# Decays of a gated DeltaNet layer from differences of running sums, with the rows spread by DMA and masked by GpSimd

## The chip, the cores and the metric

One core of a Trainium2 chip runs the whole kernel in one launch. Its engines run their own instruction streams, each in order: TensorE (PE, with its weight loads as PEld), VectorE (DVE), ScalarE (ACT), GpSimd (POOL) and SyncE (SP), which here only issues transfers. The metric is the device time of one execution in microseconds (us), as the median of several runs.

## The reference

The input is x (256 tokens by 2048 features, float32). Two layers follow, each h = h + Mixer(RMSNorm(h)). The first is a gated DeltaNet layer with 16 heads of 128, the second a chunked attention with a band of nine chunks of 64 and a relative bias. The change touches the decays of the first:

```python
beta = sigmoid(b_in)
g = -exp(a_log) * softplus(a_in + dt_bias)     # a gate per token and head
gc = cumsum(g)                                 # the reference restarts it in chunks of 64
decay = exp(where(tri_incl, gc[..., :, None] - gc[..., None, :], -inf))
lower = where(tri_strict, (k * beta) @ k.T * decay, 0)
qk = (q @ k.T) * decay
```

Decays therefore depend only on differences of the running sums of g. The kernel works on blocks of 128 tokens: for each head it holds three 128x128 blocks of decays, from tokens of the first half to the first half, from the first half to the second, and from the second half to the second. The first and the last are zero on the wrong side of the diagonal.

## The kernel before

Nearly all of the time goes into four projections. Their weights are read once, in a `plan` of 320 chunks of 512 KB. For each chunk, `fetch` issues a DMA from SP into a buffer `wt` (four of them); ACT rounds it to `whi` (L209, three buffers), and DVE takes the rest, `wlo` = `wt` - `whi` (L210, three buffers). PE then multiplies with both (L259): in a chunk of the kind "half", eight matmuls of 512 columns with `whi` and eight of 256 columns with `wlo`, and every second chunk starts with `wlo`. `fetch` runs up to three chunks ahead of use (`LOOK = 3`), but a cast into `whi` can start only when PE has finished with the buffer three chunks back.

All other work is written as generators (`decays`, `conv`, `q_conv`, `q_rest`, `k_small`, `inversion` and so on), put into two lists, `bgq` and `bg2`. After a certain number of matmuls, `step` advances one of them by one `yield`. From the resulting program, a scheduler with a timeline model then sets the order on each engine when the kernel is built; on the chip that order is fixed.

`decays` runs on `bg2` during the projection of q (from 33 to 109 us in the profile). It computes beta and the gates g (`q` in the code, 128 tokens by 16 heads by 2 halves). Then it forms the running differences as matrix products. DVE multiplies a 128x128 lower triangle `lt_f` by g for each head into `rbuf` (L486), in a rounded part and a rest (`g_r`, `gl_r`, made at L475 and L476). PE multiplies these with a strict triangle `gt_r` or with ones, `ones_r` (L501): three products for each of four groups of heads, each in two parts of 512 columns. ACT takes the exponentials out of PSUM into `dec`, a part of the tile `dl` (L506, L507 in width 512, L509 in width 128 with `tail`, the last column of the first block, as bias), and DVE multiplies the two diagonal blocks by the triangle (L516).

In `q_rest`, PE transposes q by heads (L552), after a silu on ACT (L546), and ACT sums the squares (L558). `conv` scales on ACT (L527) and adds three taps on DVE (L529).

Of the kernel before, what the change touches and what calls it, by code (L numbers as in the profile page):

```python
# [7 lines left out]
F32 = mybir.dt.float32  # L8
F32R = mybir.dt.float32r
BF16 = mybir.dt.bfloat16  # L10
AF = mybir.ActivationFunctionType
ALU = mybir.AluOpType
AX = mybir.AxisListType

P = 128
D = 2048
T = 256
H = 16
KT = D // P
EPS = 1e-6  # L20
NEG = -1e30
# [18 lines left out]
def tile_hybrid_trunk(  # L40
# [11 lines left out]
    nc = tc.nc  # L52
    act, dve, pool, pe = nc.scalar, nc.vector, nc.gpsimd, nc.tensor

    const = ctx.enter_context(tc.tile_pool(name="const", bufs=1))
# [3 lines left out]
    tiny = ctx.enter_context(tc.tile_pool(name="tiny", bufs=2))  # L59
# [3 lines left out]
    def ps_small():  # L63
        return pss.tile([P, 512], F32, name="pss", tag="pss")
# [5 lines left out]
    def slot(tag, kb, dt=F32):  # L70

        return big.tile([P, kb * 256], dt, name=tag, tag=tag)
# [5 lines left out]
    abm = slot("kT", 16)  # L78
# [5 lines left out]
    ps = ps_small()  # L84
    for _ in range(NWARM):
# [6 lines left out]
                       pattern=[[-1, P]], channel_multiplier=1)  # L92
    lt_f = abm[:, 1024:1024 + P]
    pool.memset(lt_f, 1.0)
    pool.affine_select(out=lt_f, in_=lt_f, compare_op=ALU.is_ge, fill=0.0, base=0,
                       pattern=[[1, P]], channel_multiplier=-1)
    gt_f = abm[:, 1024 + P:1024 + 2 * P]
    pool.memset(gt_f, 1.0)
    pool.affine_select(out=gt_f, in_=gt_f, compare_op=ALU.is_gt, fill=0.0, base=0,
                       pattern=[[-1, P]], channel_multiplier=1)  # L100
    ones_f = const.tile([P, P], F32, name="ones_f")
    pool.memset(ones_f, 1.0)
    nhalf = const.tile([P, 16], F32, name="nhalf")
    pool.memset(nhalf, -0.5)
    gt_r = const.tile([P, P], F32R, name="gt_r")
    ones_r = const.tile([P, P], F32R, name="ones_r")

    def rsqrt(dst, src, scale, bias):

# [298 lines left out]
    def ht(name, dt=F32):  # L408
        return const.tile([P, H, 2], dt, name=name)

    beta, g_r, gl_r = ht("beta"), ht("g_r", F32R), ht("gl_r", F32R)

    dl = slot("dl", 48).rearrange("p (h k c) -> p h k c", h=H, k=2)
    dec = dl[:, :, 1, :]
# [3 lines left out]
        return dl[:, 4 * k:4 * k + 4, 0, :].rearrange("p h (b d) -> p h b d", d=P)[:, :, 0::2, :]  # L418

    def decays():  # L420
        act.copy(out=gt_r, in_=gt_f)
        act.copy(out=ones_r, in_=ones_f)

        abr = slot("tt", 16, F32R)[:, :KT * 64 + 64]
        abv = abr[:, :KT * 64].rearrange("p (j a c) -> p j a c", a=2, c=32)
        act.copy(out=abr[:, KT * 64:], in_=ident[:, :64])
# [4 lines left out]
        ps = ps_small()  # L431
# [9 lines left out]
        ps = ps_small()  # L441
# [7 lines left out]
        for t in range(2):  # L449
            dve.tensor_scalar(out=ab[:, :, t], in0=ab[:, :, t], scalar1=rx[:, t:t + 1],  # L450
                              scalar2=None, op0=ALU.mult)

        y, ay, e, z, w2, q, eb = (abm[:, 1600 + 32 * i:1632 + 32 * i].rearrange("p (h t) -> p h t", t=2)
                                  for i in range(7))
# [13 lines left out]
        for n in (15, 13, 11, 9, 7, 5, 3):  # L468
# [3 lines left out]
        dve.scalar_tensor_tensor(out=q, in0=q, scalar=2.0, in1=y, op0=ALU.mult, op1=ALU.add)  # L472
        dve.scalar_tensor_tensor(out=q, in0=q, scalar=-1.0, in1=nea.unsqueeze(2).broadcast_to([P, H, 2]),
                                 op0=ALU.mult, op1=ALU.mult)
        dve.tensor_copy(out=g_r, in_=q)  # L475
        dve.tensor_tensor(out=gl_r, in0=q, in1=g_r.bitcast(F32), op=ALU.subtract)  # L476
        yield 1
        dve.tensor_scalar(out=eb, in0=eb, scalar1=1.0, scalar2=None, op0=ALU.add)
        dve.reciprocal(out=beta, in_=eb)

        rbuf = slot("tt", 16, F32R).rearrange("p (b k c) -> p b k c", b=2, k=4)

        def rhs(gi):
            for half in range(2):
                for part, src in ((0, g_r), (1, gl_r)):
                    dve.tensor_tensor(  # L486
                        out=rbuf[:, gi % 2, 2 * half + part, :].rearrange("p (h c) -> p h c", h=4),
                        in0=lt_f.unsqueeze(1).broadcast_to([P, 4, P]),
                        in1=src[:, 4 * gi:4 * gi + 4, half].bitcast(F32).unsqueeze(2).broadcast_to([P, 4, P]),
                        op=ALU.mult)  # L490

        rhs(0)
        yield 1
        rhs(1)
        yield 1
        for gi in range(4):
            hs = slice(4 * gi, 4 * gi + 4)
            ps3 = [ps_small() for _ in range(3)]
            for dst, lhs, half in ((ps3[0], gt_r, 0), (ps3[1], ones_r, 1), (ps3[2], gt_r, 1)):
                for part in range(2):  # L500
                    pe.matmul(dst, lhsT=lhs, rhs=rbuf[:, gi % 2, 2 * half + part, :],  # L501
                              start=(part == 0), stop=(part == 1))
            v0 = ps3[0].rearrange("p (h c) -> p h c", h=4)
            tail = tiny.tile([P, 4], F32, name="tail", tag="tail")
            dve.tensor_copy(out=tail, in_=v0[:, :, P - 1])
            act.activation(out=dec[:, hs, 0:128], in_=v0, func=AF.Exp)  # L506
            act.activation(out=dec[:, hs, 256:384], in_=ps3[2].rearrange("p (h c) -> p h c", h=4), func=AF.Exp)  # L507
            for i in range(4):
                act.activation(out=dec[:, 4 * gi + i, 128:256], in_=ps3[1][:, i * P:(i + 1) * P], func=AF.Exp,  # L509
                               bias=tail[:, i:i + 1])  # L510
            yield 1
            if gi < 2:
                rhs(gi + 2)
            yield 1
            for c in (0, 256):
                dve.tensor_tensor(out=dec[:, hs, c:c + 128], in0=dec[:, hs, c:c + 128],  # L516
                                  in1=lt_f.unsqueeze(1).broadcast_to([P, 4, P]), op=ALU.mult)
            yield 1

    def conv(src, i0):  # L520

# [402 lines left out]
    for gi in range(4):  # L924
        ps = pair(xb, 2)
# [212 lines left out]
    for gi in range(4):  # L1138
        c = 1024 * (gi % 2)
# [109 lines left out]
```

## Time and profile before

| | |
|---|---|
| median of 3 runs | 1008.43 us (1008.25 to 1009.47) |
| the profiled execution | 1010.83 us |
| its span in the profile | 1009.1 us |
| granted TensorE clock, mean | 0.997 |
| PE busy | 1001.4 us (99%) |
| DVE, ACT, POOL busy | 690.0, 526.6, 62.4 us |

The profile is one execution. A line of a timeline gives the start, the time in which the group was busy, the engine, the line of the code, the operation, what it writes and reads (buffer numbers left out), the shapes and the count; in brackets stands the idle time before it and what ended it. A line of the waits says who waited for whom: total, times, longest. A line of a table of windows gives a stretch, its length, and the busy time of each engine with its count of instructions, then the granted TensorE clock (1.00 is full speed), the busy share of the DMA engines and GB/s. Matmuls of a row overlap, so that starts say more than busy times.

### The profile page before, as it was taken

To read this page: it belongs to the slowest core of one execution; us is meant where nothing else is said; L and a number is where in the kernel's file an instruction comes from. 1 tells how busy PE (TensorE), PEld (TensorE's weight loads), DVE (VectorE), ACT (ScalarE), POOL (GpSimd) and SP (SyncE) were. 2 spreads that over 40 slices of the span, in tenths; PEclk is the share of its full clock that TensorE was granted. 3 is DMA by queue.
4 is the path that set the end of the run, shared out by engine and by line. 5 is a ranking of instruction groups with operands and counts; after the bars stand their busy time and mean duration, and the time that the engine had idled before them with its cause. 6 is when DMAs were issued, how large, how long until landed. Compare 5 with 4: busy or idle time off the path is not lost.

```text
span 1009.1 us, 15660 instructions
## 1 busy us (share of the span) xinstructions
PE 1001.4 (99%) x6090; PEld 878.8 (87%) x6090; DVE 690.0 (68%) x1121; ACT 526.6 (52%) x784; POOL 62.4 (6%) x83
## 2 busy tenths in 40 slices
PE   8999999999999999999999999999999999999998
PEld 7988888888888899899988888888888888889987
DVE  5789979997998767755867555444456666666554
ACT  6557865565446555534645444444445555555432
POOL 1000001022000000001000000000011010101000
PEclk8999999999999999999999999999999999999999
DMA  8665565555665454535765776666665565554472
GB/s 285 169 169 167 158 185 145 160 160 167 197 186 163 131 148 145 167 127 180 237 188 183 224 219 204 193 191 194 199 186 169 148 178 155 167 157 157 158 230 92
DMA packets 134186, 177.57 MB, mean 176 GB/s; under 512 B 7904, under 2 KB 90208, under 8 KB 134112
## 3 DMA queue, kind: packets, MB, share of 16 engines
q1 hardware_dynamic: 132672, 172.12, 57.5%
q0 software_dynamic: 1152, 4.19, 1.2%
q8 instruction: 47, 0.77, 0.3%
q10 hardware_dynamic: 288, 0.26, 0.1%
q14 instruction: 27, 0.22, 0.1%
HBM read 174.46 MB, written 2.10 MB: 175 GB/s over the span
## 4 chain that ended last, share of the span: by engine, by line
PE 98%; DMA 1%; DVE 0%; ACT 0%; issue 0%; SPq 0%
PE psp L259 87%; PE pss L601 2%; PE pss L259 1%; PE pss L1068 1%; DMA wt<-in_a_w_in_dram 1%; PE pss L1087 1%; PE pss L1123 1%; PE pss L833 1%; PE pss L501 1%; PE pss L1113 1%; PE pss L857 0%; PE pss L856 0%; PE pss L840 0%; PE pss L858 0%; PE pss L1086 0%; PE pss L1124 0%
## 5 line engine op out<-in xcount | busy, mean ns | idle before, releaser
L210 DVE TENSOR_TENSOR wlo<-wt,whi 128x1024 fp32r<-128x1024 f32 (+1 forms) x322 | 391.2, 1218 | 244.9 <-ACT whi L209 241.0
L209 ACT CAST whi<-wt 128x1024 fp32r<-128x1024 f32 (+1 forms) x322 | 336.7, 1046 | 381.3 <-PE psp L259 331.8
L259 PE MATMUL psp<-whi,xb 128*128 128x512 f32 x1024 | 318.9, 391 | 0.0
L259 PE MATMUL psp<-xb,whi 128*128 128x512 f32 (+1 forms) x1088 | 261.4, 382 | 2.2 <-ACT whi L209 1.9
L259 PEld LDWEIGHTS psp<-xb,whi 128*128 128x128 f32 x1088 | 197.0, 191 | 36.4 <-ACT whi L209 2.5
L259 PEld LDWEIGHTS psp<-whi,xb 128*128 128x128 f32 x1024 | 191.7, 188 | 39.1
L259 PE MATMUL psp<-wlo,xb 128*128 128x512 f32 x512 | 200.8, 392 | 0.0
L259 PE MATMUL psp<-xb,wlo 128*128 128x256 f32 x1024 | 149.0, 285 | 0.7 <-DVE wlo L210 0.7
L259 PE MATMUL psp<-g,whi 128*128 128x256 f32 (+1 forms) x736 | 149.6, 318 | 0.0
L259 PEld LDWEIGHTS psp<-xb,wlo 128*128 128x128 f32 x1024 | 138.0, 192 | 6.6 <-DVE wlo L210 1.2
L259 PEld LDWEIGHTS psp<-g,whi 128*128 128x128 f32 x736 | 121.7, 191 | 8.4 <-DVE g L900 0.2
L259 PEld LDWEIGHTS psp<-wlo,xb 128*128 128x128 f32 x512 | 96.2, 188 | 19.7
L259 PE MATMUL psp<-g,wlo 128*128 128x256 f32 x480 | 101.9, 284 | 0.3 <-DVE wlo L210 0.3
L259 PEld LDWEIGHTS psp<-g,wlo 128*128 128x128 f32 x480 | 77.8, 191 | 1.7 <-DVE wlo L210 0.5
L529 DVE SCALAR_TENSOR_TENSOR cv<-raw,sm,cv 128x255 f32<-128x255 f32 (+2 forms) x144 | 63.8, 477 | 3.4 <-ACT cv L527 3.2
L527 ACT ACTIVATE cv<-raw,sm 128x256 f32<-128x256 f32 x48 | 22.5, 509 | 20.6 <-DVE raw L345 20.6
L1051 POOL TENSOR_SCALAR ssn<-ssn,uh 128x4 f32<-128x4 f32 x16 | 8.3, 530 | 266.8 <-DVE ssn L1049 266.8
L330 DVE TENSOR_TENSOR ev<-psp,ev 128x512 f32<-128x512 f32 x33 | 22.6, 684 | 0.1
L329 ACT COPY ev<-psp 128x512 f32<-128x512 f32 x33 | 19.1, 579 | 0.0
L1099 ACT ACTIVATE raw<-raw,mx 128x128 f32<-128x128 f32 (+1 forms) x32 | 14.2, 446 | 7.4 <-DVE mx L1097 7.4
L605 DVE TENSOR_TENSOR dl<-pss,dl 128x512 f32<-128x512 f32 (+1 forms) x32 | 16.3, 551 | 2.7 <-PE pss L601 2.7
L1058 DVE TENSOR_TENSOR cv<-psp,rn 128x512 f32<-128x512 f32 x16 | 10.2, 683 | 8.9 <-POOL rn L1053 8.9
(233 smaller groups left out, 742.4 us busy)
## 6 DMA issues: line engine op xcount, KB each, us to landing
wt<-in_b_w_in_dram SPq DMA_DIRECT2D x128, 512.0 KB, 3.7
wt<-in_a_w_in_dram SPq DMA_DIRECT2D x127, 512.0 KB, 4.0
wt<-in_a_w_out_dram SPq DMA_DIRECT2D x32, 512.0 KB, 3.8
wt<-in_b_w_out_dram SPq DMA_DIRECT2D x32, 512.0 KB, 3.9
dl<-in_xT_dram POOLq DMA_DIRECT2D x4, 512.0 KB, 5.8
dl<-in_relb_dram POOLq DMA_DIRECT2D x4, 512.0 KB, 4.9
g<-in_xT_dram SPq DMA_DIRECT2D x7, 256.0 KB, 5.2
out_dram<-cv SPq DMA_DIRECT2D x2, 512.0 KB, 3.5
```

What stands on the lines that cost most here:

```text
L209: cast = act.copy(out=hi[:, js, cs], in_=wt[:, js, cs])
L210: rest = dve.tensor_tensor(out=lo[:, js, cs], in0=wt[:, js, cs], in1=hi[:, js, cs].bitcast(F32), op=ALU.subtract)
L259: state["mm"] = pe.matmul(*args, **kw).ins
L329: act.copy(out=ev, in_=ps[:, :, 1, :])
L330: dve.tensor_tensor(out=ev, in0=ps[:, :, 0, :], in1=ev, op=ALU.add)
L501: pe.matmul(dst, lhsT=lhs, rhs=rbuf[:, gi % 2, 2 * half + part, :], start=(part == 0), stop=(part == 1))
L527: act.activation(out=cv[:, i, :], in_=raw[:, i, :], func=AF.Copy, scale=conv_w(i0 + i, 3))
L529: dve.scalar_tensor_tensor(out=cv[:, i, s:], in0=raw[:, i, :T - s], scalar=conv_w(i0 + i, 3 - s), in1=cv[:, i, s:], op0=ALU.mult, op1=ALU.add)
L601: pe.matmul(dst, lhsT=kq[:, a, i, c:c + P], rhs=rhs, start=(n == 0), stop=(n == 2))
L605: dve.tensor_tensor(out=dl[:, h, :, c], in0=src.rearrange("p (k c) -> p k c", k=2), in1=dec[:, h, c].unsqueeze(1).broadcast_to([P, 2, n]), ...
L1058: dve.tensor_tensor(out=n[:, t, :].rearrange("p (h d) -> p h d", d=P), in0=ps[:, t, :].rearrange("p (h d) -> p h d", d=P), in1=rn[:, t, :] ...
L1099: act.activation(out=s[:, a:b], in_=s[:, a:b], func=AF.Exp, bias=mx[:, t:t + 1], accum_out=sums[:, t:t + 1])
```

## The change

The running sums are now computed once, by two small float32 products of g (128 tokens by 32) with the triangle: one gives the sums as 32 rows of 128, the other as 128 rows of 32. The second is negated into `ngc`, the bias column of the exponentials. The first is copied to SBUF, written to a DRAM tile `line` (16 KB) and read back by four DMAs that spread each row to all 128 partitions, into `gb` (in the tile `tt`). GpSimd copies each diagonal block from `gb` to `dec` with the wrong side filled by -1e30, four heads at a time (eight `affine_select`), and ACT takes the exponential in place, head by head, with `ngc` as bias. The block between the halves is taken straight from `gb`, with `across` (the last sum of the first half plus `ngc`) as bias. The 24 products of L501, the 16 of L486 on DVE and the 8 masks of L516 are gone, with their operands.

```diff
-        dve.tensor_copy(out=g_r, in_=q)
-        dve.tensor_tensor(out=gl_r, in0=q, in1=g_r.bitcast(F32), op=ALU.subtract)
-        yield 1
+        gf = q.rearrange("p h t -> p (h t)")
         dve.tensor_scalar(out=eb, in0=eb, scalar1=1.0, scalar2=None, op0=ALU.add)
         dve.reciprocal(out=beta, in_=eb)
-        rhs(0)
-        yield 1
-        rhs(1)
+        yield 1
+        ps = ps_small()
+        pe.matmul(ps[0:32, 0:P], lhsT=gf, rhs=lt_f, start=True, stop=True)
+        pe.matmul(ps[:, P:P + 32], lhsT=lt_f, rhs=gf, start=True, stop=True)
+        grow = abm[0:32, 1280:1280 + P]
+        dve.tensor_copy(out=grow, in_=ps[0:32, 0:P])
+        ngc = const.tile([P, H, 2], F32, name="ngc")
+        dve.tensor_scalar(out=ngc, in0=ps[:, P:P + 32].rearrange("p (h t) -> p h t", t=2), scalar1=-1.0, scalar2=None,
+                          op0=ALU.mult)
+        line = rows.tile([32, P], F32, name="line")
+        nc.gpsimd.dma_start(out=line, in_=grow)
+        gb = slot("tt", 16).rearrange("p (j c) -> p j c", c=P)
+        for gi in range(4):
+            js = slice(8 * gi, 8 * gi + 8)
+            nc.gpsimd.dma_start(out=gb[:, js, :], in_=line[js, :].unsqueeze(0).broadcast_to([P, 8, P]))
+        yield 1
+        gb = gb.rearrange("p (h t) c -> p h t c", t=2)
+        across = const.tile([P, H], F32, name="across")
+        dve.tensor_tensor(out=across, in0=gb[:, :, 0, P - 1], in1=ngc[:, :, 0], op=ALU.add)
         yield 1
         for gi in range(4):
             hs = slice(4 * gi, 4 * gi + 4)
-            ps3 = [ps_small() for _ in range(3)]
-            for dst, lhs, half in ((ps3[0], gt_r, 0), (ps3[1], ones_r, 1), (ps3[2], gt_r, 1)):
-                for part in range(2):
-                    pe.matmul(dst, lhsT=lhs, rhs=rbuf[:, gi % 2, 2 * half + part, :],
-                              start=(part == 0), stop=(part == 1))
-            v0 = ps3[0].rearrange("p (h c) -> p h c", h=4)
-            tail = tiny.tile([P, 4], F32, name="tail", tag="tail")
-            dve.tensor_copy(out=tail, in_=v0[:, :, P - 1])
-            act.activation(out=dec[:, hs, 0:128], in_=v0, func=AF.Exp)
-            act.activation(out=dec[:, hs, 256:384], in_=ps3[2].rearrange("p (h c) -> p h c", h=4), func=AF.Exp)
-            for i in range(4):
-                act.activation(out=dec[:, 4 * gi + i, 128:256], in_=ps3[1][:, i * P:(i + 1) * P], func=AF.Exp,
-                               bias=tail[:, i:i + 1])
-            yield 1
-            if gi < 2:
-                rhs(gi + 2)
-            yield 1
-            for c in (0, 256):
-                dve.tensor_tensor(out=dec[:, hs, c:c + 128], in0=dec[:, hs, c:c + 128],
-                                  in1=lt_f.unsqueeze(1).broadcast_to([P, 4, P]), op=ALU.mult)
-            yield 1
+            for t in range(2):
+                pool.affine_select(out=dec[:, hs, 2 * P * t:2 * P * t + P], in_=gb[:, hs, t, :], compare_op=ALU.is_ge,
+                                   fill=NEG, base=0, pattern=[[0, 4], [1, P]], channel_multiplier=-1)
+            for h in range(4 * gi, 4 * gi + 4):
+                act.activation(out=dec[:, h, P:2 * P], in_=gb[:, h, 1, :], func=AF.Exp, bias=across[:, h:h + 1])
+            yield 1
+            for h in range(4 * gi, 4 * gi + 4):
+                for t in range(2):
+                    c = 2 * P * t
+                    act.activation(out=dec[:, h, c:c + P], in_=dec[:, h, c:c + P], func=AF.Exp,
+                                   bias=ngc[:, h, t:t + 1])
+                if h % 2:
+                    yield 1
```

The scheduler sets another order around this place. In the lists below a name's number is that of its tile: in the changed kernel a chunk's number is 14 lower (whi_1153 is now whi_1139), and its line numbers differ (L203 is the cast, L253 the projection's matmul, L538 a transpose, L532 the silu, L513 the convolution's scaling).

ACT, before, from one cast of weights over three more, during the exponentials:

```order
L209 CAST whi_1112<-wt_1111 128x1024
L506 ACTIVATE dl_112<-pss_701 128x4x128
L509 ACTIVATE dl_112<-pss_702,tail_710 128x128 x4
L209 CAST whi_1153<-wt_1152 128x1024
L506 ACTIVATE dl_112<-pss_742 128x4x128
L509 ACTIVATE dl_112<-pss_743,tail_751 128x128 x4
L209 CAST whi_1193<-wt_1192 128x1024
L507 ACTIVATE dl_112<-pss_744 128x4x128
L527 ACTIVATE cv_1127<-raw_1124,sm_76 128x256 x2
L209 CAST whi_1228<-wt_1227 128x1024
```

ACT, now, from the cast of whi_1098 (formerly whi_1112), which stands just ahead, to that of whi_1179 (formerly whi_1193); g is the silu of q for the next transposes:

```order
L501 ACT_TABLE_LOAD
L501 ACTIVATE dl_108<-dl_108,ngc_680 128x128 x16
L203 CAST whi_1139<-wt_1138 128x1024
L513 ACTIVATE cv_1113<-raw_1110,sm_76 128x256 x2
L501 ACTIVATE dl_108<-dl_108,ngc_680 128x128 x7
L496 ACTIVATE dl_108<-tt_684,across_693 128x128 x12
L501 ACTIVATE dl_108<-dl_108,ngc_680 128x128
L496 ACTIVATE dl_108<-tt_684,across_693 128x128 x4
L501 ACTIVATE dl_108<-dl_108,ngc_680 128x128 x8
L532 ACT_TABLE_LOAD
L532 ACTIVATE g_897<-cv_1113 128x1024
L203 CAST whi_1179<-wt_1178 128x1024
```

The exponentials now stand in two bursts, of 16 and of 32, with one cast between them. The 16 squares of L558, which stood behind the exponentials, now stand ahead of the cast of whi_1075 (formerly whi_1089).

PE, before, in the chunks of the same stretch:

```order
L259 MATMUL psp_1110<-xb_108,whi_1089 128x512 x8
L501 MATMUL pss_744<-tt_684,gt_r_106 128x512 x2
L501 MATMUL pss_783<-tt_684,gt_r_106 128x512 x2
L259 MATMUL psp_1110<-xb_108,wlo_1090 128x256 x8
L259 MATMUL psp_1249<-xb_108,whi_1153 128x512 x7
L501 MATMUL pss_784<-tt_684,ones_r_107 128x512 x2
L259 MATMUL psp_1249<-xb_108,whi_1153 128x512
L501 MATMUL pss_785<-tt_684,gt_r_106 128x512 x2
```

PE, now, from the last chunk ahead of whi_1139 on:

```order
L253 MATMUL psp_1096<-xb_104,wlo_1099 128x256 x8
L253 MATMUL psp_1096<-xb_104,whi_1098 128x512 x8
L253 MATMUL psp_1235<-xb_104,whi_1139 128x512 x8
L253 MATMUL psp_1235<-xb_104,wlo_1140 128x256 x8
L538 MATMUL pss_1161<-ident_93,g_897 128x128 x4
L538 MATMUL pss_1188<-ident_93,g_897 128x128 x4
L253 MATMUL psp_1235<-xb_104,wlo_1180 128x256 x8
L253 MATMUL psp_1235<-xb_104,whi_1179 128x512 x8
```

The products of L501 are gone from between the chunks. The two new products stand earlier in the projection, after five matmuls of wlo_963 (formerly wlo_977), followed there by twelve transposes of the first heads; eight transposes, which read g, now stand between wlo_1140 and wlo_1180.

POOL's list, now, is: the DMA to `line`, the four DMAs from it, the eight `affine_select`, then epq as before. On SP nothing moves. On DVE `across`, which waits for all four DMAs, stands ahead of the subtraction for wlo_1140.

More of the change, by code (lines that the diff above doesn't have):

```diff
@@ L96, in tile_hybrid_trunk @@
                        pattern=[[1, P]], channel_multiplier=-1)
[L97 to L100, printed above, removed]
     ones_f = const.tile([P, P], F32, name="ones_f")
@@ L104, in tile_hybrid_trunk @@
     pool.memset(nhalf, -0.5)
-    gt_r = const.tile([P, P], F32R, name="gt_r")
-    ones_r = const.tile([P, P], F32R, name="ones_r")
     def rsqrt(dst, src, scale, bias):
@@ L409, in ht @@
         return const.tile([P, H, 2], dt, name=name)
-    beta, g_r, gl_r = ht("beta"), ht("g_r", F32R), ht("gl_r", F32R)
+    beta = ht("beta")
+    rows = ctx.enter_context(tc.tile_pool(name="rows", bufs=1, space=bass.MemoryType.DRAM))
     dl = slot("dl", 48).rearrange("p (h k c) -> p h k c", h=H, k=2)
@@ L420, in decays @@
     def decays():
-        act.copy(out=gt_r, in_=gt_f)
-        act.copy(out=ones_r, in_=ones_f)
         abr = slot("tt", 16, F32R)[:, :KT * 64 + 64]
@@ L474, in decays @@
                                  op0=ALU.mult, op1=ALU.mult)
-        dve.tensor_copy(out=g_r, in_=q)
-        dve.tensor_tensor(out=gl_r, in0=q, in1=g_r.bitcast(F32), op=ALU.subtract)
-        yield 1
+        gf = q.rearrange("p h t -> p (h t)")
         dve.tensor_scalar(out=eb, in0=eb, scalar1=1.0, scalar2=None, op0=ALU.add)
         dve.reciprocal(out=beta, in_=eb)
[L481 to L490, printed above, removed]
-        rhs(0)
-        yield 1
-        rhs(1)
+        yield 1
+        ps = ps_small()
[16 more added lines that the diff above has]
+        dve.tensor_tensor(out=across, in0=gb[:, :, 0, P - 1], in1=ngc[:, :, 0], op=ALU.add)
         yield 1
```

## The prediction

> **What bounds the kernel now.** I read the page's engine totals and its chain that ended last, then the waits, then the timelines of TensorE (PE), ScalarE (ACT) and VectorE (DVE) around 80 us, where the decays are computed, and last the rows of single operations.
>
> ```profile
> span 1009.1 us, 15660 instructions
> PE 1001.4 (99%) x6090; PEld 878.8 (87%) x6090; DVE 690.0 (68%) x1121; ACT 526.6 (52%) x784; POOL 62.4 (6%) x83
> PE 98%; DMA 1%; DVE 0%; ACT 0%; issue 0%; SPq 0%
> PE psp L259 87%; PE pss L601 2%; PE pss L259 1%; PE pss L1068 1%; DMA wt<-in_a_w_in_dram 1%; PE pss L1087 1%; PE pss L1123 1%; PE pss L833 1%; PE pss L501 1%; PE pss L1113 1%; PE pss L857 0%; PE pss L856 0%; PE pss L840 0%; PE pss L858 0%;
> ...
> ACT whi L209 <- PE psp L259: 331.8, 214, 5.1
> PE psp L259 <- ACT whi L209: 1.9, 1, 1.9
> ```
>
> PE is 98% of the chain, so a matmul taken out of it is worth its full issue time. The waits show why it never pauses: ACT's casts of weights (whi) wait for PE to free a buffer 214 times, while PE waited for a cast once. That holds only as long as ACT, which issues in order, reaches each cast in time. Both sides of the change follow from it: matmuls go away, and work arrives on ACT between two casts.
>
> **PE's issue times.**
>
> ```profile
> 43.95 0.61 PE L387 MATMUL pss<-dg,ones_f 128*128 128x128 f32 x4
> 44.31 0.36 PE L435 MATMUL pss<-xb,tt 128*128 128x256 f32 x1
> 71.55 3.82 PE L259 MATMUL psp<-xb,whi 128*128 128x512 f32 x16
> 75.20 2.08 PE L259 MATMUL psp<-xb,wlo 128*128 128x256 f32 x16
> 77.11 3.82 PE L259 MATMUL psp<-xb,whi 128*128 128x512 f32 x16
> 80.77 1.84 PE L259 MATMUL psp<-xb,wlo 128*128 128x256 f32 x14
> 94.20 1.08 PE L501 MATMUL pss<-tt,gt_r 128*128 128x512 f32 x4
> 95.12 1.10 PE L259 MATMUL psp<-xb,wlo 128*128 128x256 f32 x8
> ```
>
> Matmuls overlap, so I take starts. Sixteen with whi and sixteen with wlo, two chunks of weights, run from 71.55 to 77.11: 2.78 us a chunk, 1.83 for its whi half and 0.95 for its wlo half. Four decay matmuls run from 94.20 to 95.12, 0.23 each.
>
> *Removed from PE:* 24 of these (four groups, three products, two parts): 24 x 0.23 = 5.5 us, all on the path. *Added to PE:* two small float32 products. The float32 products of L387 appear as two instructions for each call, and four instructions take 0.36 us (43.95 to 44.31, 0.09 each): two calls, 0.4 us. A wider reading, 0.23 each as the 512-column ones, would be 0.9, a lower one nothing. Their input is ready: the last step of the gates ends on DVE at 77.9 (next fence), PE reaches them at 80.77 + 5 x 0.12 = 81.4. Without any other effect: -5.1 us.
>
> **What arrives on ACT.** ACT's and DVE's rows:
>
> ```profile
> 75.69 1.06 ACT L546 ACTIVATE g<-cv 128x1024 f32<-128x1024 f32 x1 [0.53 <-DVE kT L469]
> 76.66 1.03 ACT L209 CAST whi<-wt 128x1024 fp32r<-128x1024 f32 x1
> ...
> 80.97 1.05 ACT L209 CAST whi<-wt 128x1024 fp32r<-128x1024 f32 x1 [0.71 <-PE psp L259]
> 85.87 1.05 ACT L209 CAST whi<-wt 128x1024 fp32r<-128x1024 f32 x1 [3.85 <-PE psp L259]
> 86.82 0.58 ACT L329 COPY ev<-psp 128x512 f32<-128x512 f32 x1
> 87.42 1.28 ACT L507 ACT_TABLE_LOAD   x1
> ...
> 89.21 0.90 ACT L527 ACTIVATE cv<-raw,sm 128x256 f32<-128x256 f32 x2
> 90.01 1.04 ACT L209 CAST whi<-wt 128x1024 fp32r<-128x1024 f32 x1
> ...
> 94.08 1.13 ACT L509 ACTIVATE dl<-pss,tail 128x128 f32<-128x128 f32 x4
> 95.08 1.07 ACT L209 CAST whi<-wt 128x1024 fp32r<-128x1024 f32 x1
> ...
> 110.14 0.27 ACT L558 ACTIVATE sj<-pss 128x128 f32<-128x128 f32 x1
> ...
> 110.40 0.27 ACT L558 ACTIVATE sj<-pss 128x128 f32<-128x128 f32 x1
> ...
> 772.53 0.40 ACT L1099 ACTIVATE raw<-raw,mx 128x128 f32<-128x128 f32 x1
> 772.84 0.18 ACT L1099 ACTIVATION_READ_ACCUMULATOR raw<-raw,mx 128x1 f32 x1
> ...
> L210 DVE TENSOR_TENSOR wlo<-wt,whi 128x1024 fp32r<-128x1024 f32 (+1 forms) x322 | 391.2, 1218 | 244.9 <-ACT whi L209 241.0
> ...
> 77.67 0.19 DVE L473 SCALAR_TENSOR_TENSOR kT<-kT 128x32 f32<-128x32 f32 x1
> ```
>
> Start to start: a cast 0.95 (85.87 to 86.82), the copy 0.6, a table load 1.28, two convolution steps 0.8 (89.21 to 90.01), the silu 0.97, a square 0.25. The new exponentials are 48 of 128x128, each with a bias column, read from SBUF. Two rows bound them: L509's, bias but from PSUM, 0.25 (four from 94.08 to 95.08); L527's, a column operand and SBUF but 256 wide, 0.40. Nearest is L1099, an exponential of 128x128 from SBUF with a bias column, whose next instruction starts 0.31 later. I take 0.31: 14.9 us. What matters is the order: before, no more than a wide exponential and four small ones stand between neighbouring casts here; now 16 stand between whi_1098 and whi_1139, and 32, with two convolution steps, a table load and a silu, between whi_1139 and whi_1179.
>
> *ACT's clock.* Up to the cast at 80.97 (whi_1053) the order is as before. Then come 16 squares, moved up with their transposes, from 82.3: 4.0 + 0.8 for two convolution steps = 87.1. whi_1075 to 88.05, copy to 88.65, whi_1098 to 89.6, table load to 90.9.
>
> *The first exponential's data.* Its chain is a copy on DVE (82.1, after PE's products), a DMA of 16 KB to DRAM, four broadcasts of 512 KB, and a GpSimd (POOL) mask.
>
> ```profile
> q0 software_dynamic: 1152, 4.19, 1.2%
> ...
> dl<-in_relb_dram POOLq DMA_DIRECT2D x4, 512.0 KB, 4.9
> ...
> sm<-in_small_dram SPq DMA_DIRECT2D x1, 16.0 KB, 2.2
> ...
> L95 POOL TENSOR_SCALAR_AFFINE_SELECT kT<-kT 128x128 f32<-128x128 f32 x1 | 0.3, 287 | 0.0
> ```
>
> 16 KB landed in 2.2 us from the SP queue and 512 KB in 4.9 from POOL's, so the write is between 2.2 and 4.9; I take 3.4, nearer the one of its size: 85.5. First broadcast: 90.4. A mask of 128x512 is between 0.29 (width costs nothing) and four times that, 1.15; I take 0.9, as most of such a time follows the width. First exponential at 91.3. Sixteen at 0.31 end at 96.3; the masks keep up, one in 0.9 against four exponentials in 1.24. Later broadcasts share the engines: queue q0's 4.19 MB took 1.2% of 16 engines' span, 12 us, so 2.1 MB needs 6 us of all engines, or 12 at half. The second pair of masks then comes at most 1.1 us late; I take 0.
>
> Then: whi_1139 0.95, convolution 0.8, 32 exponentials 9.9, table load 1.28, silu 0.97: whi_1179 starts at 110.2, is done at 111.3, and DVE's 1.2 us for wlo_1180 (L210's row) gives 112.5.
>
> *PE's clock.* From 81.4: products 0.4, twelve transposes at 0.09 1.1, rest of the chunk 0.3, whi_1006's chunk 2.8 with four transposes 0.3: 86.3. Chunks 1031, 1053, 1075, 1098 end at 97.4; whi_1139 is there at about 97.3, so no stall yet; its chunk ends at 100.2. The next rows, eight transposes (0.7 us) of the silu's output and then wlo_1180, wait for ACT until 112.5. Stall: 112.5 - 100.2 - 0.7 = 11.6 us. Queued behind it on PE is all the rest of the program.
>
> **The clock after the stall.** The one longer pause of before is at the start:
>
> ```profile
> 10.00:12.00 2.00, 0.78 (x2) 0.50 (x2) 1.00 (x2) 1.81 (x3) 0.27 (x1) 0.69 1.06 393
> 12.00:14.00 2.00, 1.54 (x8) 1.52 (x8) 1.55 (x4) 1.55 (x4) 0.25 (x1) 0.50 1.04 369
> ...
> 16.00:18.00 2.00, 2.00 (x13) 2.00 (x12) 1.87 (x3) 1.24 (x2) 0.81 (x2) 0.61 1.05 310
> ...
> 12.48 0.58 PE L259 MATMUL psp<-xb,wlo 128*128 128x256 f32 x1 [0.46 <-DVE wlo L210]
> ```
>
> In these windows (PEclk is the third number from the right) the granted clock falls to 0.50 around a pause of about 2 us, and steady matmuls from 12.48 run at half speed for 78% of the last window, to 17.6: 5.1 us at half speed, 2.5 us lost. The stall is longer than that pause, so I add 2.5; bounds are 0 and 3.4 (half speed over 62% of the first window, from 10.8, to 17.6 is 6.8 us).
>
> [...]
>
> **Costed at nothing.** DVE loses 24 operations (16 products into tt, 8 masks); it is not on the path. POOL's five DMAs and eight masks stand ahead of only one operation for the rest of this stage, epq, which is needed only after the inversion. The weight queue on SP keeps its order. Two ACT casts and two POOL operations at the start go, under PE's work. If the casts' cover failed later too, ACT would be late again; after whi_1179 two casts follow at once, so I see none.
>
> **Sum.** -5.5 + 0.4 + 11.6 + 2.5 = +9.0 us. The profiled execution took 1010.83 us for its span of 1009.1; its span would become 1018.1. It lies 2.4 us above the median of the runs, 1008.43, to which I add the difference: 1017.4.
>
> **Rivals.** *Covered burst, faster:* the exponentials fit under the chunks already cast, and only -5.1 remains: 1003.3. For it: ACT's waits of up to 5.1 us for PE. Against: that cushion is two to three chunks, while the second burst alone is 13.9 us. It decides if the 48 exponentials take under 0.07 each (11.6 us less); no row is so quick. *No change:* stall and clock together give back just 5.1: exponentials of 0.17 and a clock that stays, 48 x 0.14 = 6.7 off the stall. The squares' 0.25 speaks against it. *Clock stays:* 1014.9, which a stall broken into pieces would give. *POOL is the bound:* a mask held up by DVE. Rows of one operation:
>
> ```profile
> 807.29 1.57 POOL L1051 TENSOR_SCALAR ssn<-ssn,uh 128x4 f32<-128x4 f32 x2 [25.81 <-DVE ssn L1049]
> 831.33 0.51 POOL L1051 TENSOR_SCALAR ssn<-ssn,uh 128x4 f32<-128x4 f32 x2 [20.75 <-DVE ssn L1049]
> ```
>
> The same pair took 0.51 or 1.57, so a mask may be 1.1 longer, 2.0: four of them end at 98.4 instead of 94.0 and ACT's chain shifts from 96.3 to 99.6: 1020.7. Against: with ACT stuck, DVE has little to run. [...]
>
> **How the numbers follow.** Main forecast 0.50 (its own range 1014 to 1020), clock stays 0.18, POOL bound 0.15, later still (slow broadcasts) 0.04, no change 0.06, covered 0.07. Low end: exponentials of 0.25 (48 x 0.06 = 2.9 less) and no clock loss: 1012.0, rounded to 1011.5. High end: POOL 3.3, broadcasts 1.1, clock 0.9 on top: 1022.7, rounded to 1023. A measurement of this kernel tells 0.2%, 2 us, from no change: slower 0.87, same 0.06, faster 0.07.
>
> **What would show it.** In the profile of the changed kernel: PE waiting for ACT's silu or whi once, 10 to 13 us, around 100 us; ACT without idle time from 91 to 111; a PEclk digit below 9 near 110; exponentials 0.31 apart; masks 0.9 long; no L501 matmuls of 512 columns. The forecast is wrong if PE shows no wait there, or if the masks or broadcasts, not ACT, end the wait.

## The result and the profile after

The changed kernel takes 1017.34 us (median of 4 runs, 1016.42 to 1019.09) against 1008.61 for the kernel before in the same series: a ratio of 1.0085 (95% interval 1.0073 to 1.0098), slower by 8.7 us. A second series gave 1018.09 against 1008.77, 1.0086 (1.0072 to 1.0101). The prediction was 1017.4. The profiled execution took 1019.09 us, so it is 1.75 above its median; the three others are 1.2 to 2.7 shorter than it.

From the page of the changed kernel (span, busy time of the engines with count of instructions, and the chain that ended last by engine):

```profile
span 1017.4 us, 15640 instructions
PE 998.2 (98%) x6070; PEld 875.1 (86%) x6070; DVE 676.9 (67%) x1094; ACT 531.8 (52%) x806; POOL 69.6 (7%) x94
...
PE 94%; ACT 2%; issue 1%; DVE 1%; DMA 1%; SPq 0%; POOL 0%; DVEq 0%; POOLq 0%
```

PE is busy 3.2 us less than before and is still later: its part of the chain fell from 98% to 94%, and ACT, which had 0%, has 2%, some 20 us. Where PE waited is in its list of waits (total, times, longest):

```profile
PE pss L538 <- ACT g L532: 9.4, 1, 9.4
PE psp L253 <- ACT whi L203: 2.9, 2, 1.8
PE psp L253 <- DVE wlo L204: 1.6, 4, 0.8
```

One wait of 9.4 us is new, and it is the transposes that wait for a silu on ACT. The timeline of PE shows its place, and what follows it:

```profile
79.50 0.41 PE L472 MATMUL pss<-kT 128*32 128x128 f32 x2
79.84 0.41 PE L473 MATMUL pss<-kT 128*128 128x32 f32 x2
80.08 1.51 PE L538 MATMUL pss<-ident,g 128*128 128x128 f32 x12
...
94.34 2.00 PE L253 MATMUL psp<-xb,whi 128*128 128x512 f32 x8
98.17 2.14 PE L253 MATMUL psp<-xb,whi 128*128 128x512 f32 x8 [1.83 <-ACT whi L203]
100.15 1.10 PE L253 MATMUL psp<-xb,wlo 128*128 128x256 f32 x8
110.69 1.97 PE L538 MATMUL pss<-ident,g 128*128 128x128 f32 x8 [9.45 <-ACT g L532]
112.89 2.08 PE L253 MATMUL psp<-xb,wlo 128*128 128x256 f32 x8 [0.23 <-DVE wlo L204]
114.76 4.94 PE L253 MATMUL psp<-xb,whi 128*128 128x512 f32 x16
119.54 2.08 PE L253 MATMUL psp<-xb,wlo 128*128 128x256 f32 x16
```

Three losses show: 1.83 us ahead of whi_1139's matmuls, 9.45 ahead of the transposes, and slow matmuls behind the second wait. Eight matmuls with wlo_1180 take 1.87 us from start to start (112.89 to 114.76) where eight took 0.95 before, and sixteen with whi take 4.78 where sixteen took 3.65: together 2.05 us lost at half the clock. From 119.54 on all is as it was.

ACT in the same stretch:

```profile
88.17 1.28 ACT L501 ACT_TABLE_LOAD   x1
92.39 4.79 ACT L501 ACTIVATE dl<-dl,ngc 128x128 f32<-128x128 f32 x16 [2.93 <-POOL dl L493]
97.09 1.03 ACT L203 CAST whi<-wt 128x1024 fp32r<-128x1024 f32 x1
...
98.83 2.14 ACT L501 ACTIVATE dl<-dl,ngc 128x128 f32<-128x128 f32 x7
100.89 3.60 ACT L496 ACTIVATE dl<-tt,across 128x128 f32<-128x128 f32 x12
...
105.85 2.43 ACT L501 ACTIVATE dl<-dl,ngc 128x128 f32<-128x128 f32 x8
108.29 1.28 ACT L532 ACT_TABLE_LOAD   x1
109.58 1.06 ACT L532 ACTIVATE g<-cv 128x1024 f32<-128x1024 f32 x1
110.55 2.92 ACT L203 CAST whi<-wt 128x1024 fp32r<-128x1024 f32 x3
```

Both bursts are there, of 16 and of 32, at 0.295 us an exponential (sixteen from 92.39 to 97.09). ACT idles 2.93 us for the first mask and then not at all until 110.55. What the first mask waited for stands on POOL, and in the rows of the new DMAs (count, KB each, median time from issue to landing):

```profile
80.86 0.74 POOL L480 DMA_DIRECT2D line<-kT  x1 [42.58 <-DVE ngc L477]
84.66 2.13 POOL L484 DMA_DIRECT2D tt<-line  x4 [3.05 <-ACT sj L544]
91.71 2.49 POOL L493 TENSOR_SCALAR_AFFINE_SELECT dl<-tt 128x512 f32<-128x512 f32 x4 [4.92 <-DMA tt<-line]
```

```profile
tt<-line POOLq DMA_DIRECT2D x4, 512.0 KB, 8.2
...
line<-kT POOLq DMA_DIRECT2D x1, 16.0 KB, 3.2
```

The broadcasts are issued at 84.66, when the write to DRAM, issued at 80.86 and 3.2 us to landing, has been through for 0.6 us. The bracket names ACT's squares; in the second profile of this kernel (below) it names another row, and the issue again comes 0.6 us behind the landing, so it is the write that is waited for. The first broadcast lands at 91.7, 7.0 us after its issue, and the masks take 0.62 us each.

One thing in this pair of profiles is not of the change. PE starts the chunk of wlo ahead of the products at 78.82 here and at 80.77 before, mainly because the profiled execution of before ran at half clock from 10.7 to 17.6 us and this one did not. From that chunk to the first product of k (L601 at 157.78 before, L587 at 166.17 now) it took 77.0 us before and 87.4 now: 10.3 us more, while the medians differ by 8.7. Behind that point every common row is 8.3 to 8.4 us later, so nothing more is lost or won there.

### The profile page after: what moved, and what is told of

It is laid out like the page before. It is cut to its first block, busy times and chain, and to the rows that moved or that the text cites. A ratio compares the mean times of both kernels' runs of the same rounds, so it can differ in the third digit from the quotient of the medians.

```text
span 1017.4 us, 15640 instructions
## 1 busy us (share of the span) xinstructions
PE 998.2 (98%) x6070; PEld 875.1 (86%) x6070; DVE 676.9 (67%) x1094; ACT 531.8 (52%) x806; POOL 69.6 (7%) x94
## 4 chain that ended last, share of the span: by engine, by line
PE 94%; ACT 2%; issue 1%; DVE 1%; DMA 1%; SPq 0%; POOL 0%; DVEq 0%; POOLq 0%
PE psp L253 83%; PE pss L587 2%; ACT dl L501 1%; PE pss L253 1%; PE pss L1054 1%; PE pss L1073 1%; PE pss L1109 1%; DMA wt<-in_a_w_in_dram 1%; PE pss L819 1%; DVE wlo L204 1%; PE pss L1099 1%; ACT dl L496 0%; ACT whi L203 0%; ACT sj L544 0%; PE pss L842 0%
## 5 line engine op out<-in xcount | busy, mean ns | idle before, releaser
L203 ACT CAST whi<-wt 128x1024 fp32r<-128x1024 f32 (+1 forms) x322 | 336.3, 1046 | 380.8 <-PE psp L253 327.6
L253 PE MATMUL psp<-whi,xb 128*128 128x512 f32 x1024 | 319.3, 392 | 0.0
L253 PE MATMUL psp<-xb,whi 128*128 128x512 f32 (+1 forms) x1088 | 259.6, 382 | 3.7 <-ACT whi L203 2.9
L253 PEld LDWEIGHTS psp<-xb,whi 128*128 128x128 f32 x1088 | 196.1, 190 | 38.6 <-ACT whi L203 3.9
L253 PEld LDWEIGHTS psp<-whi,xb 128*128 128x128 f32 x1024 | 191.8, 188 | 39.2
L253 PE MATMUL psp<-wlo,xb 128*128 128x512 f32 x512 | 201.0, 393 | 0.0
L253 PE MATMUL psp<-g,whi 128*128 128x256 f32 (+1 forms) x736 | 149.6, 319 | 0.1
L253 PE MATMUL psp<-xb,wlo 128*128 128x256 f32 x1024 | 148.4, 286 | 1.2 <-DVE wlo L204 1.2
L253 PEld LDWEIGHTS psp<-xb,wlo 128*128 128x128 f32 x1024 | 137.4, 192 | 7.4 <-DVE wlo L204 2.2
L253 PEld LDWEIGHTS psp<-g,whi 128*128 128x128 f32 x736 | 121.7, 191 | 8.4 <-DVE g L886 0.3
L253 PEld LDWEIGHTS psp<-wlo,xb 128*128 128x128 f32 x512 | 96.2, 188 | 19.4
L253 PE MATMUL psp<-g,wlo 128*128 128x256 f32 x480 | 102.0, 284 | 0.3 <-DVE wlo L204 0.3
L253 PEld LDWEIGHTS psp<-g,wlo 128*128 128x128 f32 x480 | 77.8, 192 | 1.7 <-DVE wlo L204 0.5
L513 ACT ACTIVATE cv<-raw,sm 128x256 f32<-128x256 f32 x48 | 22.5, 508 | 22.5 <-DVE raw L339 22.5
L855 POOL TENSOR_TENSOR ro<-so,nhalf 128x8 f32<-128x8 f32 x4 | 6.5, 1636 | 156.0 <-DVE so L853 156.0
```

Of the source, the lines that this page charges most:

```text
L203: cast = act.copy(out=hi[:, js, cs], in_=wt[:, js, cs])
L253: state["mm"] = pe.matmul(*args, **kw).ins
L513: act.activation(out=cv[:, i, :], in_=raw[:, i, :], func=AF.Copy, scale=conv_w(i0 + i, 3))
```

## The experiments

Theory A: ACT works in order, and its bursts of exponentials stand ahead of a cast and a silu that PE needs; the stall, with the half clock behind it, is the whole loss, and the matmuls taken out are worth their 5.1 us. Theory B: the data are late (write, broadcasts, masks), whatever their order on ACT. Theory C: something costed at nothing (POOL, DMA traffic, DVE's order) takes part of it.

### More work in the burst, less on PE

The repeated exponentials:

```diff
                 act.activation(out=dec[:, h, P:2 * P], in_=gb[:, h, 1, :], func=AF.Exp, bias=across[:, h:h + 1])
+                act.activation(out=dec[:, h, P:2 * P], in_=gb[:, h, 1, :], func=AF.Exp, bias=across[:, h:h + 1])
```

> Each of the 16 exponentials of the block between the halves is issued twice (the second writes the same values again). In ACT's order 13 of the 16 repeats fall into the second burst, 3 behind the cast after it with one more pair of table loads. Theory A: PE's second wait grows by 13 x 0.295 = 3.8 us, 9.45 to 13.3: 1021.2, up to 1022.5 if the three late ones and their table load cost too. Theory B: the repeats need no new data, the time stays at 1017.3 (within 0.5).

Measured: 1021.47 us (1.0124 of before, 1.0110 to 1.0138), 4.1 above the changed kernel. PE's timeline:

```profile
112.84 1.97 PE L539 MATMUL pss<-ident,g 128*128 128x128 f32 x8 [13.24 <-ACT g L533]
```

The wait grew from 9.45 to 13.24, by 3.8 as 13 exponentials at 0.295 give. What is put into that burst goes to the end of the program at its full length: theory A. No data were later, so B does not give it.

Half of the old matrix products:

```diff
-                for part in range(2):
-                    pe.matmul(dst, lhsT=lhs, rhs=rbuf[:, gi % 2, 2 * half + part, :],
-                              start=(part == 0), stop=(part == 1))
+                pe.matmul(dst, lhsT=lhs, rhs=rbuf[:, gi % 2, 2 * half, :], start=True, stop=True)
```

> The kernel before with one of the two parts of its matrix products left out: the rest g - round(g) is not multiplied, so 12 of the 24 matmuls of 512 columns are gone and the decays carry the rounded gates only. It prices the matmuls alone. If each is worth its 0.23 us of issue: 12 x 0.23 = 2.8 us less, 1005.8. If PE's time there is limited by the weights or casts anyway: no change, 1008.5.

Measured: 1006.17 us against 1008.6, ratio 0.9970 (0.9959 to 0.9982): 2.4 us less, with 1.8 to 4.1 in the interval, which holds the 2.8. The matmuls were worth what their issue says.

### The same work in another order

In the next kernels the exponentials are issued in groups, each behind the cast of a new chunk of weights; n is the size of a group and s the number of casts that pass before the first. Only the order changes. The first had n = 3, s = 7:

```diff
-        yield 1
+        for _ in range(7):
+            yield from new_cast()
...
+        for n0 in range(0, len(todo), 3):
+            yield from new_cast()
+            with behind_cast():
+                for o, i, b in todo[n0:n0 + 3]:
+                    act.activation(out=o, in_=i, func=AF.Exp, bias=b)
```

> Same 48 narrow exponentials, same eight masks and the same five DMAs as in the changed kernel, but the exponentials are started later and issued three behind each cast of weights (a first group of 8 and one of 4 + 2 + 7 remain, with one more pair of table loads). Theory A (the loss is ACT's burst: 32 exponentials in front of one cast): no PE wait above 2 us near 100 us, the 5.1 us of removed matmuls come through: 1003.5, up to 1006 because the 7.1 us of ACT work ahead of one cast are more than a chunk's 2.78. Theory B (the loss is late data: DRAM write, broadcasts, masks): the first exponentials still wait for the masks with casts behind them, PE waits 5 us or more: 1009 to 1017.

Measured: 1008.05 us, 0.9993 of before (0.9984 to 1.0001): 9.3 us better than the changed kernel, and no gain on before. Neither theory had it right. PE's and ACT's timelines of this kernel:

```profile
97.83 3.30 PE L253 MATMUL psp<-xb,whi 128*128 128x512 f32 x8 [1.99 <-ACT whi L203]
```

```profile
93.60 1.28 ACT L517 ACTIVATE dl<-dl,ngc 128x128 f32<-128x128 f32 x4 [4.01 <-POOL dl L505]
```

ACT stands 4.01 us for the first mask with the cast behind it, PE waits 1.99 us, and eight matmuls then take 3.14 us (97.83 to 100.97) in place of 1.83. A second wait on a cast, of 1.07 us at 107.32, is a burst once more: nine exponentials, two table loads and a silu stand on ACT between that cast and the one before. So late data do cost, where the first exponential stands too early in ACT's order; in the changed kernel the burst is the larger part (9.45 us against 1.83). The half clock belongs to the profiled execution, 1.4 us above the median: in eight of the eleven executions of this kernel the mean granted clock is 1.000.

The wide form, started early (n = 1 of 512 columns, s = 3):

```diff
+                dve.tensor_tensor(out=o, in0=gb[:, hs, src, :], in1=bias.unsqueeze(2).broadcast_to([P, 4, P]), op=ALU.add)
+                if b != 1:
+                    pool.affine_select(out=o, in_=o, compare_op=ALU.is_ge,
+                                       fill=NEG, base=0, pattern=[[0, 4], [1, P]], channel_multiplier=-1)
+                with behind_cast():
+                    act.activation(out=o, in_=o, func=AF.Exp)
```

> The bias is added by DVE (twelve additions of 128x512 with the column spread along the row), GpSimd masks in place, and ACT takes twelve exponentials of 128x512 without bias, two behind each cast. Theory A: ACT has 12 x about 0.65 = 8 us instead of 14.2, spread over six casts: no PE wait above 1 us, 1003.5 (1002.5 to 1005). Theory B (late data): the chain is longer here (an addition of 0.6 us ahead of every mask), so PE would wait as long as in the changed kernel or longer: 1015 to 1019. A third outcome, DVE held up at its additions by the broadcasts with the subtractions for wlo behind them: PE waits on wlo, 1005 to 1010.

Measured: 1011.54 us, 1.0026 of before (1.0017 to 1.0034); the third outcome, a little above its range. PE and DVE:

```profile
103.34 2.00 PE L253 MATMUL psp<-xb,wlo 128*128 128x256 f32 x8 [3.35 <-DVE wlo L204]
```

```profile
94.36 1.29 DVE L507 TENSOR_TENSOR dl<-tt,ngc 128x512 f32<-128x512 f32 x2 [1.17 <-DMA tt<-line]
```

DVE waits for broadcasts at its additions, 1.88 us ahead of the first pair and 1.17 ahead of the second, and its subtractions for wlo stand behind those and behind more additions of 0.6 us each; PE waits 1.30 and then 3.35 us for them. So the same mistake is made on another engine.

Now the same two forms with s = 15: the first exponential stands four casts later than in the changed kernel, when masks and broadcasts are done.

> The changed kernel with its 48 exponentials started four casts later, when masks and broadcasts are long done, and four of them behind each cast of weights; work and data are those of the changed kernel. Theory A (burst ahead of a cast): ACT has 0.95 + 4 x 0.295 = 2.1 us a chunk against PE's 2.78, so no PE wait above 0.5 us, the clock stays at 1.00, and only the 5.1 us of the matmuls remain: 1003.5 (1002.5 to 1004.5). Theory B (data late by itself costs): also 1003.5, since no data is late here. Theory C (something else in the change costs about 4 us: POOL, DMA traffic, DVE order): 1007 to 1009, as with the interleaved kernel before.

> As with four behind each cast, but sixteen behind each of three casts; the first starts at the same place, with its data there. Theory A: up to the first of these casts PE has three chunks (8.3 us) in hand, then two groups follow with 0.95 + 4.7 + 0.5 us against 2.78 each: waits of about 0.2, 3.4 and 2.9 us, and about 2 us of half clock: 1003.5 + 8.5 = 1012 (1009 to 1013.5). Theory B (late data): no wait, 1003.5.

> As before, but all 48 exponentials in one burst behind one cast. Theory A: from that cast's start to the end of the next 0.95 + 1.28 + 14.2 + 2 (squares between) + 0.95 = 19.4 us against three chunks of 8.3: PE waits once, about 11 us, and loses about 2 us of clock: 1003.5 + 13 = 1016.5 (1014.5 to 1018). Theory B (late data): no wait, 1003.5.

> The wide form (DVE adds the bias, GpSimd masks in place, twelve exponentials of 128x512 on ACT), started four casts later and one behind each cast. Theory A with data in time: ACT has 0.95 + 0.65 = 1.6 us a chunk, DVE 1.2 + 0.6 = 1.8, both under 2.78: no PE wait above 0.5 us, 1003.5 (1002.5 to 1004.5). If DVE's additions hold up wlo as in the earlier wide kernel: 1006 to 1011.

| kernel | us, median | ratio to before (95%) | expected by A | by B |
|---|---|---|---|---|
| four behind each cast | 1005.94 | 0.9972 (0.9961 to 0.9983) | 1003.5 | 1003.5 |
| sixteen behind each | 1012.59 | 1.0033 (1.0021 to 1.0046) | 1012 | 1003.5 |
| all 48 behind one | 1016.97 | 1.0082 (1.0068 to 1.0096) | 1016.5 | 1003.5 |
| wide, one behind each | 1003.48 | 0.9949 (0.9936 to 0.9963) | 1003.5 | not given |

With the data in time, the time grows with the length of the burst. PE's timelines, of the kernel with sixteen and then of the one with 48:

```profile
117.62 2.08 PE L253 MATMUL psp<-xb,wlo 128*128 128x256 f32 x8 [4.32 <-DVE wlo L204]
```

```profile
119.08 3.62 PE L253 MATMUL psp<-xb,whi 128*128 128x512 f32 x8 [11.15 <-ACT whi L203]
122.54 2.07 PE L253 MATMUL psp<-xb,wlo 128*128 128x256 f32 x16
```

The wait of 11.15 stands against about 11 expected. With sixteen, three waits of 0.2, 3.4 and 2.9 us were expected; in this stage the profile has two, 4.32 and 1.01, so the median fits better than the parts. Theory C falls with the wide kernel: it has the five DMAs, eight masks and twelve more operations on DVE, and its 1003.48 is 5.2 us under before, so all those cost nothing measurable (the interval, 3.7 to 6.5 us gained, leaves room for 1.4 of the 5.1 expected). It is also the version that beats both kernels. A table of windows of that kernel shows PE busy throughout and POOL's masks (fifth engine column) beside it:

```profile
108.00:112.00 4.00, 4.00 (x26) 3.57 (x25) 4.00 (x6) 3.37 (x6) 1.56 (x1) 1.00 0.46 137
120.00:124.00 4.00, 4.00 (x27) 3.64 (x26) 4.00 (x8) 3.38 (x5) 0.82 (x1) 1.00 0.56 160
```

The kernel with four behind each cast came out 2.4 us above its forecast, though its profiled execution (1004.34 us, its fastest) has PE as busy. Two runs looked for the reason: three behind each cast, and the same kernel once more.

> As with four behind each cast, but three, over sixteen casts. With four, ACT was busy 38.5 us out of 40 in the stretches looked at, and its executions lay between 1004.3 and 1007.1. If that spread comes from ACT being full (any delay reaches PE): with three, ACT has 0.3 us less per chunk, and the median falls to 1003.5 to 1004.5. If it comes from the start of the program (pauses of PE before 20 us, which differ from execution to execution): the same 1005.9.

> The kernel with four exponentials behind each cast, for a second profile: its executions lay between 1004.3 and 1007.1, and the one profiled was the fastest. If ACT being nearly full is the cause, a longer execution shows PE waiting for whi or wlo between 100 and 140 us, 0.5 to 2 us, with a half-speed stretch behind it. If the start is the cause, it shows half speed between 8 and 20 us alone, and no wait above 0.3 us later.

Three behind each: 1009.9 us, 1.0007 of before (0.9998 to 1.0016). Neither reason gives a slower kernel. In its profile PE waits for nothing between 20 and 430 us; beside the start, new waits stand far from the change, in a later projection, each with another, of 0.95 and 0.83 us, close behind it:

```profile
436.71 0.50 PE L253 MATMUL psp<-g,whi 128*128 128x256 f32 x2 [1.02 <-ACT whi L203]
...
470.33 0.50 PE L253 MATMUL psp<-g,whi 128*128 128x256 f32 x2 [0.73 <-ACT g L901]
```

Its sixteen groups last until 145 us, and the small products of k wait for them when the order is made; the scheduler then set the work of the next 300 us in another order. Rows common with the four-each kernel are 1.2 us later from the start on, and 4.5 from 733 us on. So this run says nothing of ACT's load, and three behind each cast is slower than four for another reason than its burst: a reordering is not local. The repeat of the four-each kernel: 1005.67 us (1005.31 to 1007.16), profiled at 1005.31, its lowest:

```profile
140.75 1.22 PE L253 MATMUL psp<-xb,wlo 128*128 128x256 f32 x8 [0.34 <-DVE wlo L204]
```

No wait in this stage is longer than that. It is 0.98 us later than the first profile, 0.85 of it from the start of the program, where it runs at half clock between 12.1 and 15.6 us; so far as these two profiles go, that speaks for the start. Why some executions reach 1007 no profile shows. It is not the clock alone, as the mean granted clock is 0.998 in the repeat's executions of 1005.31 and of 1007.16 alike; the cause stays open.

### The clock behind the wait

In the kernel with 48 in one burst, 44 matmuls whose results are not used were put on PE ahead of the wait:

```diff
+                    ps = ps_small()
+                    for _ in range(44):
+                        pe.matmul(ps, lhsT=xb[:, 0, 0, 0:P], rhs=xb[:, 0, :, :], start=True, stop=True)
```

> The kernel with all 48 exponentials in one burst, and 44 matmuls of 512 columns on data already there (results not used) put on PE between the halves of the last whi but one ahead of its wait of 11.2 us: 44 x 0.23 = 10.1 us, so that PE is kept busy up to about 1 us before the cast comes. If the pause drops the clock: the granted clock stays at 1.00, the 1.6 us lost at half speed after the pause come back, 1015.4. If the loss has nothing to do with the pause: 1017.0 as without the filling. If PE's work ahead of the wait does lie on the path after all: 1025 or more.

Measured: 1014.44 us (1.0053 of before, 1.0040 to 1.0066) with 10.1 us more work on PE than the 1016.97 of the same burst without it. PE, and a window of the same profile:

```profile
105.13 10.14 PE L523 MATMUL pss<-xb 128*128 128x512 f32 x44
```

```profile
118.00:120.00 2.00, 1.92 (x9) 1.24 (x7) 0.17 (x1) 2.00 (x8) 0.00 (x0) 1.00 0.00 0
```

The granted clock (third number from the right) stays at 1.00 and PE has no wait above 0.2 us there. Over its five executions the mean granted clock is 0.997 to 1.000, against 0.991 to 0.995 over the four without the filling. The added work costs nothing, and 2.5 us come back: here the pause drops the clock (half speed from 112.14 to 122.38 us without the filling), and this wait costs more than its length. Not all of the 2.5 is clock. From the start of the whi matmuls among which the filling stands to that of the whi matmuls two groups on (100.38 to 124.45 without it, 102.40 to 123.91 with it) the two profiles differ by 2.56 us; 1.63 of that is the half speed, the 1.6 expected. For the rest, ACT's burst starts 1.1 us earlier against PE's chunk in the filled profile, so that there was less to wait for.

A second profile of the changed kernel:

> The changed kernel as it is, for a second profile: its profiled execution was 1.75 us above its median, and in it the stretch from the products to the first product of k took 10.3 us more than before, against 8.7 between the medians. If half speed comes in steps of 3.4 us on a grid that stands at a different place in each execution, a second profile shows a half-speed stretch of 6.8, 10.2 or 13.6 us and another loss behind the wait (0.4 to 3.4 us), with the waits themselves the same (about 1.8 and 9.5); the median stays at 1017.3. If the clock falls at a fixed delay after the pause begins: the same 2.3 us after it, and the same 2.05 us lost.

Measured: 1018.09 us. PE's two waits in this profile (execution of 1017.90 us):

```profile
97.26 2.14 PE L253 MATMUL psp<-xb,whi 128*128 128x512 f32 x8 [1.07 <-ACT whi L203]
...
109.79 1.97 PE L538 MATMUL pss<-ident,g 128*128 128x128 f32 x8 [9.45 <-ACT g L532]
```

The large wait is the same to 0.01 us, the one that hangs on the data fell from 1.83 to 1.07, not the same as expected, and the matmuls behind lost 1.75 us instead of 2.05. The stretch took 86.3 us, 9.3 more than before. The data came sooner behind their issue; POOL's rows:

```profile
84.94 2.13 POOL L484 DMA_DIRECT2D tt<-line  x4 [3.48 <-ACT cv L513]
90.80 2.50 POOL L493 TENSOR_SCALAR_AFFINE_SELECT dl<-tt 128x512 f32<-128x512 f32 x4 [3.73 <-DMA tt<-line]
```

Here the write took 3.6 us, the first broadcast 5.9 us to landing and the four 7.0 in the middle.

## Why the prediction was right, step by step

The sum, against what the two profiles of the changed kernel hold; the long wait is from the end of wlo_1140's matmuls to the start of wlo_1180's, less 0.8 for the transposes:

| term | predicted | first profile | second profile |
|---|---|---|---|
| 24 matmuls gone | -5.5 | -5.5 | -5.5 |
| two small products | +0.4 | +0.6 (79.50 to 80.08) | +0.6 |
| wait at whi_1139 | 0 | +1.8 | +1.1 |
| the long wait | +11.6 | +11.0 | +11.0 |
| half clock | +2.5 | +2.05 | +1.75 |
| sum | +9.0 | +10.0 | +8.9 |
| the stretch measured | | +10.3 | +9.3 |

*The matmuls.* The gain of 5.1 was there: the wide kernel, in which PE waits for nothing in this stage, got 5.2.

*The burst.* The place (the silu, and the cast behind it), the two bursts and the length were as forecast. An exponential took 0.295 us, not 0.31, 0.7 us less over 48.

*The data.* This step failed. The first exponential started at 92.39 on a clock on which PE is 1.95 us earlier than in the forecast, so 3.0 us late. The broadcasts were taken at 4.9 us, the row of other transfers of 512 KB; the first took 7.0, and the four 8.2 in the middle: 2.1 us of the delay. Another 1.1 stand ahead of them. The write itself was right (3.2 against 3.4), but it began 0.7 us later than in the forecast, behind DVE's copy and the next operation, and the broadcasts were issued 0.6 us after it landed; the forecast had no term for either. Masks of 0.62 instead of 0.9 gave 0.3 back. In the second profile the same terms are 1.5 us up to the issue and 1.0 for the first broadcast, 2.3 late in all. Hence "no stall yet" at whi_1139 was wrong, and PE waited 1.1 to 1.8 there. One sign of being wrong that the forecast named, a wait that masks or broadcasts end, thus came true for this wait (through ACT, which stood 2.93 us for the first mask), and not for the long one. Since that wait made PE late as well, the long wait behind it did not grow: the forecast of 11.6 came out at 11.0 although ACT reached whi_1179 2.3 us late (110.55), for the end of PE's chunk was 2.9 us late, 1.8 of it that wait.

*The clock.* It fell, and the loss was 0.45 and 0.75 us smaller than taken, inside its bounds.

*The rivals.* A covered burst, no change and a clock that stays are all excluded by the 9.45 us wait and the half speed behind it. POOL did not become the bound: its masks ran at 0.62 us, and what it waited for later were broadcasts. DVE stood idle for 5.4 us around them, as argued; where it was busy, in the wide kernel started late, a single operation held POOL for 1.56 us of one window (108 to 112, DVE 4.00 of 4.00). That DVE is what holds POOL up was my assumption; no run shows it. Slow broadcasts, which I gave 0.04, did happen; with the rest of the late data they were worth the 1.1 to 1.8 us of that wait and not the whole. In the second profile the errors cancel (+1.1 at whi_1139 and +0.2 for the products against -0.6 and -0.75 for the long wait and the clock); in the first, 1.0 us is left. The time is closer to the forecast than its terms deserve.

*What was costed at nothing* (DVE's 24 operations, POOL's queue, SP's order) was nothing that can be measured, by the wide kernel. The remark that a repair lies in the order and not in the work was not in the prediction; the runs show it.

## What to carry to other kernels

Before work is moved onto an engine that issues in order, count what will stand between two of its operations for which the bottleneck waits, and compare it with what the bottleneck has in hand there (8.3 us here); the engine's average load (52%) says nothing of it. Start such work only where its data are sure to be there, since a wait at the head of the group holds everything behind it (ACT stood 4.01 us so in the interleaved kernel, with the cast behind), and prefer few wide instructions: twelve exponentials of 512 columns, one behind each cast, made the same change 5.2 us faster than before instead of 8.7 slower. When the order is made by a scheduler, look at later stages too: moving a group can cost 300 us further on.

## What the runs showed of the hardware

The clock came in steps of about 3.41 us. With windows of half a microsecond the edges of the half-speed stretches can be read (a window at 0.94 was at half speed for 12% of its 0.5 us). First of the changed kernel, then of its second profile, of the interleaved kernel with the early start, and of before:

```profile
103.00:103.50 0.50, 0.00 (x0) 0.00 (x0) 0.00 (x0) 0.50 (x3) 0.00 (x0) 0.94 0.06 20
...
117.00:117.50 0.50, 0.50 (x4) 0.41 (x3) 0.00 (x0) 0.00 (x0) 0.00 (x0) 0.91 1.03 340
```

```profile
105.00:105.50 0.50, 0.00 (x0) 0.00 (x0) 0.00 (x0) 0.50 (x3) 0.00 (x0) 0.88 0.00 0
...
115.50:116.00 0.50, 0.50 (x3) 0.39 (x2) 0.00 (x0) 0.00 (x0) 0.00 (x0) 0.88 1.07 373
```

```profile
98.00:98.50 0.50, 0.50 (x3) 0.41 (x4) 0.50 (x2) 0.50 (x3) 0.26 (x1) 0.92 0.00 0
...
101.50:102.00 0.50, 0.50 (x5) 0.50 (x4) 0.50 (x1) 0.49 (x2) 0.00 (x0) 0.67 0.07 8
```

```profile
10.50:11.00 0.50, 0.00 (x0) 0.00 (x0) 0.00 (x0) 0.50 (x1) 0.27 (x1) 0.74 1.10 399
17.50:18.00 0.50, 0.50 (x6) 0.50 (x5) 0.37 (x1) 0.50 (x1) 0.41 (x1) 0.93 1.07 412
```

Half speed lasted from 103.44 to 117.09 (13.65 us), 105.38 to 115.62 (10.24), 98.42 to 101.83 (3.41) and 10.74 to 17.57 (6.83): four, three, one and two times 3.41. The clock fell 2.3 us after the pause began in one profile of the changed kernel and 5.2 us after it in the other, so the delay is not fixed; that the steps stand on a grid is a reading of these lengths, and no run shows more of it. Behind a pause of 1.99 us the clock fell in the profiled execution of the interleaved kernel, and behind the one of 1.83 us in the changed kernel it stayed at 1.00 (98 to 102 us). A stretch of 3.41 us at half speed makes a mean of 0.998 in the interleaved kernel, and eight of its eleven executions have 1.000, so in those no such stretch followed. So the loss behind a pause does not go with its length: 0.9 us behind the 13.24 of the kernel with repeated exponentials, where the clock returned at 116.8, and 2.05 behind 9.45. Half speed also sets the start of the program apart from execution to execution: 6.8 us at half speed in the profile of before, 3.4 in that with three behind each cast, none in the two of the changed kernel.

The second thing not expected: four DMAs of 512 KB from POOL, each spreading 4 KB of DRAM to 128 partitions, took 8.2 us to landing in the middle, where eight others of 512 KB from the same queue took 5.2 and 5.9 in the same profile. Over all twelve profiles with such broadcasts their medians are 6.7 to 8.6 us, those of the others 5.0 to 6.4. Whether the spreading or the transfers beside them make the difference no run here shows.
